# A two-layer encoder trunk on one core: first half of x scaled in two pieces, first two features' projections moved ahead of value products, value weights copied behind features

## The chip, the cores and the metric

The kernel runs on one core of a Trainium2 chip. A core has five engines with queues of their own: TensorE (PE in the profile; its weight loads are PEld), VectorE (DVE), ScalarE (ACT), GpSimd (POOL) and SyncE (SP, which issues nearly all transfers here). The metric is the device time of one execution in microseconds (us); smaller is better.

## The reference

Two layers act on x, 1024 positions by 1024 features, in float32. Each layer normalizes x, modulates it, mixes over positions, adds the result to x, and then does the same with a dense SwiGLU block. Only the start of layer 0 matters here:

```
mod = silu(c) @ ada_w[0] + ada_b[0]            # ada_w[0]: 1024 x 6144
sh1, sc1, g1, sh2, sc2, g2 = split(mod, 6)
h = rms_norm(x, norm1_g[0]) * (1 + sc1) + sh1
q, k, v, f_logit = split(h @ fox_w_in, ...)    # 1024 x (3*1024 + 16)
```

Forgetting attention with 16 heads follows, later gated linear attention, and a final normalization. So the first projections need the modulation vectors sh1 and sc1, and these need a third of ada_w[0], 8 MB.

## The kernel before, in words

The program is traced as straight code. A planner then orders the instructions of each engine by a simulated timeline, with the order of the code as priority; data dependences become semaphores. `tied(i, ...)` (L273) adds an order by hand: every instruction traced inside it stands behind `i` on `i`'s own engine. `last_of(e, n)` (L120) names the last instruction, or the one n before the last, traced on an engine so far. An instruction without such a tie stands wherever the planner put it.

Nearly all matrix products are done three times, on a high and a low part of each operand (`mm3`, L268): high times high, high times low, low times high. A weight is loaded raw, copied by ACT into its high part, and the low part is the difference, in four pieces (`split_w`, L208): piece i goes to POOL if i is below `lo_p` and to DVE otherwise.

"Features" below are the eight blocks of 128 columns of x. "Halves" are positions 0 to 511 and 512 to 1023. In the first stage this happens:

- `load_x`, `load_ada0`: SP issues x tiles (128 positions by 1024 columns, 512 KB), modulation weights (four transfers of 256 KB for each feature d) and projection weights into one queue. Order before: tiles 0 and 1, weights of feature 0, tiles 2 and 3, the f weight, q and k weights of the first head pair, modulation weights of features 1, 2 and 3, the first half of the value weights, modulation weights 4 and 5, the second half of the value weights, modulation weights 6 and 7, tiles 4 to 7.
- `ss_tiles` (L523): ACT squares tiles with a running sum, DVE and POOL turn the sums into 1/rms (`rstd`), and each tile is multiplied by it in place. `by` names the engine of each tile: D, A or G (POOL).
- `ada0_mod(d)` (L548): the modulation of feature d, a sum over eight chunks of 128 inputs. `NPE[d]` chunks are matmuls on PE (L557, each with one column); the others are summed on DVE (L563, L565) into `acc`, which PE reduces over partitions (L567). DVE adds the bias (L569, `modc`) and makes the multiplier (L410, `amul`).
- `h_block(d, hf)` (L573): PE transposes feature d of four tiles (L577), ACT applies multiplier and shift (L580, `y`) and makes the high part (L582), DVE or POOL makes the low part (L583).
- `first_k(d, hf, acc)` (L589): the products of feature d with the weights of f (two), q (three) and k (three), each over 512 positions, accumulated over the features in three PSUM banks.
- `first_v(d)` (L966): its twelve products with the value weights, 256 columns each, accumulated in two more banks.
- `pre(d)` (L976) is `ada0_mod`, the load for feature d + 3 and `h_block(d, 0)`.

The loop over d (L985) calls, for each d, the value weights' load and split (at d = 0 and 2), `pre(d + 1)`, `first_k(d)`, and, from d = 3 on, `first_v(d - 3)`; the second half's x tiles are loaded at d = 4 and squared and scaled at d = 4 and 5. Then the last value products, `first_evac(0)` and the second half's eight features follow. After that come value and q/k projections of further heads and attention, each on PE in turn.

Of the kernel before, what the change touches and what calls it, by code (L numbers as in the profile page):

```python
# [16 lines left out]
P = 128  # L17
# [37 lines left out]
def trunk(ctx, tc, x, c, ada_w, ada_b, norm1_g, norm2_g, ffn_w_in, ffn_w_out,  # L55
# [281 lines left out]
    def load_ada0(d):  # L337
        for kh in range(2):
            t = adr([P, 4, 2, P], F32, f"adas{d}{kh}")
            for j in range(2):  # L340
                with tied(*wv_ins if d > 3 else []):
                    nc.sync.dma_start(t[:, :, j, :], adaw[0, :, 4 * kh:4 * kh + 4, j, d, :])
                last_ada[:] = [last_of("S")]
# [179 lines left out]
    def ss_tiles(t0, n, by, ta=(), td=(), tg=(), late=()):  # L523
# [9 lines left out]
        for t, e in zip(range(t0, t0 + n), by):  # L533
            r = rstd[:, t:t + 1]
            if e == "D":
                nc.vector.tensor_scalar(xt[t], xt[t], r, None, op0=ALU.mult)
            elif e == "A":
                with tied(*late):
                    nc.scalar.activation(xt[t], xt[t], AF.Copy, scale=r)
            else:  # L540
                nc.gpsimd.tensor_scalar(xt[t], xt[t], r, 1.0, op0=ALU.mult, op1=ALU.mult)

    VLAG, XD = 3, 4
    NPE = (4, 4, 4, 2, 2, 2, 2, 2)

    mods = {}

    def ada0_mod(d):  # L548
# [3 lines left out]
        behind = [last_of("P")] if d == 1 else []  # L552
# [8 lines left out]
        for k in range(npe, 8):  # L561
            if k == npe:
                nc.vector.tensor_scalar(acc, part(k), cact[:, k:k + 1], None, op0=ALU.mult)  # L563
            else:
                nc.vector.scalar_tensor_tensor(acc, part(k), cact[:, k:k + 1], acc, op0=ALU.mult, op1=ALU.add)  # L565
# [327 lines left out]
    loads = v_loads(W, 2 * D)  # L893
# [64 lines left out]
    ss_tiles(0, 4, "DADG")  # L958
    scaled = last_of("D")
    with tied(last_of("A")):  # L960
        wf = split_w16(raw_f, "fw", wst)
        wq0, wk0 = (split_w(raw, 8, P, nm, wst) for raw, nm in zip(raw_qk, ("wq0", "wk0")))
    acc = first_acc(0)
# [12 lines left out]
    def pre(d):  # L976
        ada0_mod(d)
        if d + 3 < 8:
# [4 lines left out]
    done = {}  # L983
    pre(0)
    for d in range(8):  # L985
        if d == 0:
            feed.depth = 1
            wvs[0] = [feed.next()]
            wv_ins.append(last_of("S"))
        if d == 2:  # L990
            wvs[0].append(feed.next())
        if d < 7:
            pre(d + 1)
        first_k(d, 0, acc)
        if d >= VLAG:
            first_v(d - VLAG)
# [5 lines left out]
        if d == 4:  # L1002
            ss_tiles(4, 2, "GA", done[4]["A"], mods[5], done[4]["G"], done[5]["A"])
        if d == 5:
            ss_tiles(6, 2, "GA", done[5]["A"], mods[6], done[5]["G"], done[6]["A"])
            scaled2 = [last_of("A")]
# [8 lines left out]
    for d in range(8):  # L1015
        if d < 7:
            h_block(d + 1, 1)
        if d == 0:
            w_after.append(last_of("A"))
# [1234 lines left out]
```

## Time and profile before

| | |
|---|---|
| median of 3 runs | 2397.93 us (2396.83 to 2398.89) |
| profiled execution, its own time | 2394.36 us |
| its span in the profile | 2392.6 us |
| PE busy | 2356.5 us, 98% |
| DVE, ACT, POOL busy | 1678.7, 1190.1, 1198.1 us |
| HBM traffic | 269.25 MB read, 90.24 MB written |

All times in the profile count from the start of the span. A group "x8" in the timeline is a run of instructions of one line with the start of the first and the time from there to the end of the last. A matmul's duration includes a tail that overlaps the next matmul; the price of one in a row of matmuls is the distance of starts, which the chain of waits shows. The granted clock is the share of full speed that PE's throttle allowed in a stretch.

### The profile page before, as it was taken

Reading aid. Unit: us, or ns where it says so; the run is one execution under the profiler, and the core shown is the slowest. Engines: PE = TensorE matmul, PEld = TensorE weight load, DVE = VectorE, ACT = ScalarE, POOL = GpSimd, SP = SyncE. Lnnn points to the kernel's source line nnn. Section 1 sums busy time; section 2 is a strip of 40 time slices with the busy share of each in tenths; the row PEclk is TensorE's granted clock in tenths of the full one; section 3 lists DMA queues with packets and bytes.
Section 4 is the critical chain, followed back from the end, with each engine's and each line's share of the span. In section 5 each row is a group of like instructions: output and inputs, shape, how many; then the busy total and the mean of one; then the engine's idle time right before and its main releaser. Section 6 shows DMA issues by size and latency. Waiting matters only on the chain.

```text
span 2392.6 us, 35991 instructions
## 1 busy us (share of the span) xinstructions
PE 2356.5 (98%) x12286; PEld 2002.8 (84%) x12286; DVE 1678.7 (70%) x2797; ACT 1190.1 (50%) x2286; POOL 1198.1 (50%) x1070
## 2 busy tenths in 40 slices
PE   7999999999999999999999999999999999999998
PEld 6888888878888888888888898898888888888888
DVE  6577677676697778775788655345596766766787
ACT  5655556666554444434324766564443433345326
POOL 4234344432437778753363466563345666643262
PEclk9999999999999999999999999999999999999999
DMA  9233233133335555447665244454434534357664
GB/s 275 72 106 115 88 116 115 55 97 106 128 105 192 171 173 167 154 165 270 222 230 181 76 143 120 118 151 158 127 106 150 170 130 145 136 179 258 227 207 147
DMA packets 329408, 361.89 MB, mean 151 GB/s; under 512 B 24508, under 2 KB 253016, under 8 KB 329224
## 3 DMA queue, kind: packets, MB, share of 16 engines
q1 hardware_dynamic: 329032, 359.52, 46.5%
q8 instruction: 97, 1.59, 0.3%
q14 instruction: 87, 0.71, 0.1%
q10 hardware_dynamic: 192, 0.06, 0.0%
HBM read 269.25 MB, written 90.24 MB: 150 GB/s over the span
## 4 chain that ended last, share of the span: by engine, by line
PE 86%; ACT 3%; DVE 3%; DMA 3%; issue 2%; POOL 1%; SPq 1%; DVEq 0%; POOLq 0%; ACTq 0%
PE p_b L270 16%; PE p_b L269 16%; PE p_b L271 16%; PE o_b L1123 2%; PE t_b L1109 2%; PE qk_b L269 1%; PE qk_b L270 1%; PE qk_b L271 1%; PE s_b L1078 1%; PE s_b L1079 1%; PE gr_b L270 1%; PE gr_b L269 1%; PE gr_b L271 1%; PE vps_b L270 1%; PE vps_b L269 1%
## 5 line engine op out<-in xcount | busy, mean ns | idle before, releaser
L168 DVE TENSOR_TENSOR o_s<-xv_s,o_s 128x512 fp32r<-128x512 f32 (+1 forms) x376 | 343.1, 915 | 76.3 <-ACT o_s L167 75.5
L167 ACT CAST o_s<-xv_s 128x512 fp32r<-128x512 f32 (+1 forms) x376 | 218.8, 588 | 330.6 <-PE p_b L271 261.8
L1089 POOL TENSOR_SCALAR lp_s<-lp_s,st 128x128 f32<-128x128 f32 (+7 forms) x128 | 96.8, 761 | 294.3 <-DVE st L1088 251.9
L270 PE MATMUL p_b<-B,o_s 128*128 128x512 f32 x576 | 224.2, 389 | 0.0
L271 PE MATMUL p_b<-B,o_s 128*128 128x512 f32 x576 | 223.7, 389 | 0.0
L269 PE MATMUL p_b<-B,o_s 128*128 128x512 f32 x576 | 223.1, 389 | 0.0
L826 POOL TENSOR_TENSOR ex_s<-xv_s,xv_s 128x512 f32<-128x512 f32 (+1 forms) x64 | 87.2, 1362 | 252.1 <-DMA xv_s<-in_ffn_w_in_dram 88.7
L269 PE MATMUL p_b<-T,o_s 128*128 128x512 f32 x480 | 186.7, 389 | 0.0
L270 PE MATMUL p_b<-T,o_s 128*128 128x512 f32 x480 | 186.7, 389 | 0.0
L271 PE MATMUL p_b<-T,o_s 128*128 128x512 f32 x480 | 180.7, 389 | 0.0
L1087 ACT ACTIVATE lp_s<-lp_s,st 128x128 f32<-128x128 f32 (+7 forms) x128 | 99.5, 778 | 68.6 <-DVE st L1083 66.5
L270 PEld LDWEIGHTS p_b<-B,o_s 128*128 128x128 f32 x576 | 108.2, 188 | 22.4
L269 PEld LDWEIGHTS p_b<-B,o_s 128*128 128x128 f32 x576 | 108.1, 188 | 22.5
L271 PEld LDWEIGHTS p_b<-B,o_s 128*128 128x128 f32 x576 | 108.1, 188 | 22.3
L828 POOL TENSOR_TENSOR xv_s<-ex_s,xv_s 128x512 f32<-128x512 f32 (+1 forms) x64 | 85.5, 1335 | 59.6 <-DVE o_s L168 56.8
L167 ACT CAST pt_s<-t_b 128x512 fp32r<-128x512 f32 (+1 forms) x160 | 79.6, 547 | 69.3 <-PE t_b L1109 68.7
L1475 DVE TENSOR_TENSOR ex_s<-ex_s,p_b 128x512 f32<-128x512 f32 x140 | 94.1, 681 | 26.2 <-PE p_b L271 26.0
L220 POOL TENSOR_TENSOR w_l_s<-w__s,w_h_s 128x256 fp32r<-128x256 f32 x120 | 88.3, 767 | 48.2 <-ACT w_h_s L217 44.6
L168 DVE TENSOR_TENSOR pt_s<-t_b,pt_s 128x512 fp32r<-128x512 f32 (+1 forms) x160 | 96.6, 632 | 14.5 <-ACT pt_s L167 14.2
L447 POOL TENSOR_TENSOR ad_s<-ad_s,ad_s 128x512 f32<-128x512 f32 x62 | 88.3, 1425 | 35.1 <-ACT ad_s L445 22.7
L269 PEld LDWEIGHTS p_b<-T,o_s 128*128 128x128 f32 x480 | 90.1, 188 | 18.7
L270 PEld LDWEIGHTS p_b<-T,o_s 128*128 128x128 f32 x480 | 90.1, 188 | 18.7
(1999 smaller groups left out, 7502.2 us busy)
## 6 DMA issues: line engine op xcount, KB each, us to landing
xv_s<-in_ffn_w_in_dram SPq DMA_DIRECT2D x176, 256.0 KB, 3.2
hid_B<-x SPq DMA_DIRECT2D x70, 512.0 KB, 2.7
ad_s<-in_ada_w_dram SPq DMA_DIRECT2D x384, 64.0 KB, 2.0
hid_T<-x SPq DMA_DIRECT2D x36, 512.0 KB, 2.8
xv_s<-in_ffn_w_out_dram SPq DMA_DIRECT2D x96, 192.0 KB, 4.9
ada_s<-in_ada_w_dram SPq DMA_DIRECT2D x128, 128.0 KB, 2.6
xv_s<-in_ffn_w_out_dram SPq DMA_DIRECT2D x40, 256.0 KB, 2.8
T2o<-hid_T SPq DMA_DIRECT2D x18, 512.0 KB, 9.1
```

The source lines that it names most:

```text
L167: nc.scalar.copy(hi, src)
L168: nc.vector.tensor_sub(lo, src, hi.bitcast(F32))
L220: (nc.gpsimd if i < lo_p else nc.vector).tensor_sub(lo[:, cs], rw[:, cs], hi[:, cs].bitcast(F32))
L269: nc.tensor.matmul(ps, ah, bh, start=start, stop=False)
L270: nc.tensor.matmul(ps, ah, bl, start=False, stop=False)
L271: nc.tensor.matmul(ps, al, bh, start=False, stop=stop)
L447: nc.gpsimd.tensor_add(acc, acc, raw)
L826: nc.gpsimd.tensor_add(s1, a21, a22)
L828: nc.gpsimd.tensor_sub(a11, s1, a11)
L1087: nc.scalar.activation(lp, lp, AF.Exp, bias=mcur, scale=-1.0, accum_out=st[:, qi, 2:3])
L1089: nc.gpsimd.tensor_scalar(lp, lp, st[:, qi, 3:4], 1.0, op0=ALU.mult, op1=ALU.mult)
L1475: nc.vector.tensor_add(d, d if src is None else dest(G, src), ps)
```

## The change

1. Of tiles 0 to 3 only the first 256 columns (features 0 and 1) are scaled at first, by DVE, ACT, DVE, POOL as before. The other 768 columns follow in a new function `scale_x`: tiles 0 and 1 on ACT, 2 and 3 on POOL, behind feature 0 and behind the split of the k weights on these engines.
2. The splits of the q and k weights put two of four low pieces on DVE instead of one; the k weights are split after feature 0 instead of before.
3. Products of feature 0 are traced before `pre(1)`, those of feature 1 before `pre(2)`. The modulation matmuls of features 1 and 2 stand on PE behind the fifth-last PE instruction traced before them (the fourth of the eight products).
4. `NPE` of features 1 and 2 is 2 instead of 4. DVE's sum for a feature stands behind the sum of the feature before (for feature 1: behind feature 0's low part), and its third step behind that feature's `amul`.
5. The copies of the value weights on ACT stand behind feature 1 (first half) and feature 3 (second half). All four low pieces are on POOL. The load of modulation weights 4 is traced behind the first value load, and all loads of modulation weights are tied into one order.
6. The first value products stand on PE behind the products of feature 2.
7. The second half's x tiles are squared behind features 6 and 7 on ACT and scaled after that, by POOL, ACT, POOL, DVE (before: POOL, ACT, POOL, ACT, behind features 4 to 6).

```diff
@@ load_ada0
-                with tied(*wv_ins if d > 3 else []):
+                with tied(*wv_ins if d > 3 else [], *last_ada):
@@ ss_tiles
-    def ss_tiles(t0, n, by, ta=(), td=(), tg=(), late=()):
+    def ss_tiles(t0, n, by, ta=(), td=(), tg=(), late=(), first=D):
...
-        for t, e in zip(range(t0, t0 + n), by):
-            r = rstd[:, t:t + 1]
+        scale_x(t0, by, slice(0, first), late)
+
+    def scale_x(t0, by, cols, late=()):
+        for t, e in enumerate(by, t0):
+            x_, r = xt[t][:, cols], rstd[:, t:t + 1]
             if e == "D":
-                nc.vector.tensor_scalar(xt[t], xt[t], r, None, op0=ALU.mult)
+                nc.vector.tensor_scalar(x_, x_, r, None, op0=ALU.mult)
...
-    NPE = (4, 4, 4, 2, 2, 2, 2, 2)
-    mods = {}
+    NPE = (4, 2, 2, 2, 2, 2, 2, 2)
+    mods, summed = {}, []
@@ ada0_mod
-        behind = [last_of("P")] if d == 1 else []
+        behind = [last_of("P", 4)] if d in (1, 2) else []
...
             if k == npe:
-                nc.vector.tensor_scalar(acc, part(k), cact[:, k:k + 1], None, op0=ALU.mult)
+                with tied(*summed):
+                    nc.vector.tensor_scalar(acc, part(k), cact[:, k:k + 1], None, op0=ALU.mult)
             else:
-                nc.vector.scalar_tensor_tensor(acc, part(k), cact[:, k:k + 1], acc, op0=ALU.mult, op1=ALU.add)
+                with tied(*mods[d - 1] if d > 1 and k == npe + 2 else []):
+                    nc.vector.scalar_tensor_tensor(acc, part(k), cact[:, k:k + 1], acc, op0=ALU.mult, op1=ALU.add)
+        summed[:] = [last_of("D")]
@@ loads
-    loads = v_loads(W, 2 * D)
+    loads = [a + (ws, 4) for a in v_loads(W, 2 * D)]
@@ first stage
-    ss_tiles(0, 4, "DADG")
+    ss_tiles(0, 4, "DADG", first=256)
     scaled = last_of("D")
     with tied(last_of("A")):
         wf = split_w16(raw_f, "fw", wst)
-        wq0, wk0 = (split_w(raw, 8, P, nm, wst) for raw, nm in zip(raw_qk, ("wq0", "wk0")))
-    acc = first_acc(0)
+        wq0 = split_w(raw_qk[0], 8, P, "wq0", wst, 2)
...
-    def pre(d):
+    def pre(d, load=True):
         ada0_mod(d)
-        if d + 3 < 8:
+        if load and d + 3 < 8:
             load_ada0(d + 3)
...
+    feed.depth = 1
     pre(0)
+    summed[:] = [last_of("D")]
+    with tied(last_of("A")):
+        wk0 = split_w(raw_qk[1], 8, P, "wk0", wst, 2)
+    with tied(last_of("A"), last_of("G")):
+        scale_x(0, "AAGG", slice(256, D))
+    acc = first_acc(0)
+    first_k(0, 0, acc)
     for d in range(8):
+        if d == 1:
+            first_k(1, 0, acc)
+        if d < 7:
+            pre(d + 1, d > 0)
         if d == 0:
-            feed.depth = 1
+            w_after[:] = [last_of("A")]
             wvs[0] = [feed.next()]
             wv_ins.append(last_of("S"))
+            load_ada0(4)
         if d == 2:
+            w_after[:] = [last_of("A")]
             wvs[0].append(feed.next())
-        if d < 7:
-            pre(d + 1)
-        first_k(d, 0, acc)
+        if d > 1:
+            first_k(d, 0, acc)
+        if d == 2:
+            k2 = [last_of("P")]
         if d >= VLAG:
-            first_v(d - VLAG)
+            with tied(*k2):
+                first_v(d - VLAG)
...
-        if d == 4:
-            ss_tiles(4, 2, "GA", done[4]["A"], mods[5], done[4]["G"], done[5]["A"])
-        if d == 5:
-            ss_tiles(6, 2, "GA", done[5]["A"], mods[6], done[5]["G"], done[6]["A"])
-            scaled2 = [last_of("A")]
+        if d == 6:
+            ss_tiles(4, 2, "", done[6]["A"], mods[7], done[5]["G"])
+            ss_tiles(6, 2, "", done[7]["A"], mods[7], done[5]["G"])
+            squared = [last_of("A")]
+            scale_x(4, "GAGD", slice(0, D), squared)
...
-            w_after.append(last_of("A"))
+            w_after[:] = [last_of("A")]
```

More of the change, by code (lines that the diff above doesn't have):

```diff
@@ L532, in ss_tiles @@
             nc.gpsimd.tensor_tensor(rstd[:, cs], rstd[:, cs], mhalf[:, 0:n], op=ALU.pow)
-        for t, e in zip(range(t0, t0 + n), by):
-            r = rstd[:, t:t + 1]
+        scale_x(t0, by, slice(0, first), late)
+    def scale_x(t0, by, cols, late=()):
+        for t, e in enumerate(by, t0):
+            x_, r = xt[t][:, cols], rstd[:, t:t + 1]
             if e == "D":
-                nc.vector.tensor_scalar(xt[t], xt[t], r, None, op0=ALU.mult)
+                nc.vector.tensor_scalar(x_, x_, r, None, op0=ALU.mult)
             elif e == "A":
                 with tied(*late):
-                    nc.scalar.activation(xt[t], xt[t], AF.Copy, scale=r)
+                    nc.scalar.activation(x_, x_, AF.Copy, scale=r)
             else:
-                nc.gpsimd.tensor_scalar(xt[t], xt[t], r, 1.0, op0=ALU.mult, op1=ALU.mult)
+                nc.gpsimd.tensor_scalar(x_, x_, r, 1.0, op0=ALU.mult, op1=ALU.mult)
     VLAG, XD = 3, 4
-    NPE = (4, 4, 4, 2, 2, 2, 2, 2)
-    mods = {}
+    NPE = (4, 2, 2, 2, 2, 2, 2, 2)
+    mods, summed = {}, []
     def ada0_mod(d):
```

## The prediction

> **What bounds the kernel now.** I read the page first (busy shares, chain of waits), then the first 72 us: the table of stretches, the timeline of every engine, the chain of waits and the DMA issues. The change touches only the work of those 72 us.
>
> ```profile
> span 2392.6 us, 35991 instructions
> PE 2356.5 (98%) x12286; PEld 2002.8 (84%) x12286; DVE 1678.7 (70%) x2797; ACT 1190.1 (50%) x2286; POOL 1198.1 (50%) x1070
> PE 86%; ACT 3%; DVE 3%; DMA 3%; issue 2%; POOL 1%; SPq 1%; DVEq 0%; POOLq 0%; ACTq 0%
> ```
>
> PE is busy for 98% of the span and holds 86% of the chain, so PE runs its instructions one after another to the end, and what reaches it earlier is kept as long as nothing else becomes late. The exception is the beginning. Stretches of 3 us (columns: PE, PEld, DVE, ACT and POOL busy, granted PE clock, DMA share, GB/s):
>
> ```profile
> core 0: us, PE busy (x) PEld busy (x) DVE busy (x) ACT busy (x) POOL busy (x), PEclk, DMA share, GB/s
> 30.00:33.00 3.00, 2.98 (x11) 2.50 (x11) 2.75 (x4) 1.45 (x3) 3.00 (x4) 0.50 1.21 291
> 42.00:45.00 3.00, 1.77 (x5) 1.38 (x6) 2.86 (x6) 1.15 (x2) 1.50 (x1) 0.71 1.15 325
> 45.00:48.00 3.00, 3.00 (x16) 2.70 (x15) 2.86 (x9) 2.40 (x4) 0.00 (x0) 0.72 1.03 409
> 51.00:54.00 3.00, 3.00 (x26) 2.82 (x24) 2.89 (x4) 2.94 (x6) 2.90 (x3) 1.00 0.16 38
> ```
>
> PE does 11 instructions at clock 0.50 where it later does 26 at 1.00, and it idles at 42. DMA is full until 48 and nearly empty from 51. The timeline (start, duration, engine, line; the idle time before and its releaser in brackets) shows why features come late:
>
> ```profile
> 9.84 0.35 DVE L563 TENSOR_SCALAR acc<-adas_s,cact 128x256 f32<-128x256 f32 x1 [0.66 <-DMA adas_s<-in_ada_w_dram]
> 15.18 1.15 ACT L539 ACTIVATE xt_s<-xt_s,rstd 128x1024 f32<-128x1024 f32 x1 [1.34 <-POOL rstd L532]
> 15.18 2.29 DVE L536 TENSOR_SCALAR xt_s<-xt_s,rstd 128x1024 f32<-128x1024 f32 x2 [1.14 <-POOL rstd L532]
> 15.24 1.68 POOL L541 TENSOR_SCALAR xt_s<-xt_s,rstd 128x1024 f32<-128x1024 f32 x1
> 16.42 1.14 ACT L217 CAST wq0h_s<-wq_s 128x512 fp32r<-128x512 f32 x2
> 18.12 0.68 DVE L410 SCALAR_TENSOR_TENSOR amul<-modc,vec 128x1 f32<-128x1 f32 x1
> 18.43 3.41 PE L557 MATMUL mp_b<-cact,adas_s 128*128 128x1 f32 x16
> 18.89 0.78 ACT L580 ACTIVATE y_s<-xp_b,modc,amul 128x512 f32<-128x512 f32 x1 [0.30 <-DVE amul L410]
> 19.68 2.50 POOL L220 TENSOR_TENSOR wk0l_s<-wk_s,wk0h_s 128x256 fp32r<-128x256 f32 x3
> 19.71 0.62 ACT L582 CAST h0h<-y_s 128x512 fp32r<-128x512 f32 x1
> 21.52 1.21 DVE L583 TENSOR_TENSOR h0l<-y_s,h0h 128x512 fp32r<-128x512 f32 x1
> 22.45 0.78 PE L591 MATMUL fs_b<-h0h,fw_s 128*128 128x512 f32 x1
> 24.35 1.53 DVE L565 SCALAR_TENSOR_TENSOR acc<-adas_s,cact,acc 128x256 f32<-128x256 f32 x3
> 27.00 0.16 DVE L410 SCALAR_TENSOR_TENSOR amul<-modc,vec 128x1 f32<-128x1 f32 x1
> 29.00 1.14 ACT L217 CAST wv_0h_s<-wv_s 128x512 fp32r<-128x512 f32 x2 [8.68 <-DMA wv_s<-in_fox_w_in_dram]
> 30.64 3.24 DVE L565 SCALAR_TENSOR_TENSOR acc<-adas_s,cact,acc 128x256 f32<-128x256 f32 x3
> 32.00 0.78 PE L591 MATMUL fs_b<-h0h,fw_s 128*128 128x512 f32 x1
> 36.16 0.48 PE L591 MATMUL fs_b<-h0h,fw_s 128*128 128x512 f32 x1
> 40.45 1.05 PE L557 MATMUL mp_b<-cact,adas_s 128*128 128x1 f32 x8 [0.59 <-DVE modc L569]
> 43.23 0.79 PE L591 MATMUL fs_b<-h0h,fw_s 128*128 128x512 f32 x1 [1.28 <-ACT h0h L582]
> 46.99 0.69 DVE L583 TENSOR_TENSOR h0l<-y_s,h0h 128x512 fp32r<-128x512 f32 x1
> 70.82 0.50 PE L591 MATMUL fs_b<-h0h,fw_s 128*128 128x512 f32 x1 [0.38 <-ACT h0h L582]
> ```
>
> K(d) below means the eight products of feature d (two for f, three each for q and k); V(d) its twelve value products; mods(d) its modulation sums. L591 starts K(0) at 22.45, K(1) at 32.00, K(2) at 36.16, K(3) at 43.23, and K(0) of the second half at 70.82. Feature 0 is ready for PE at 20.33 (19.71 + 0.62), but PE is busy with the sixteen matmuls of mods(1). Feature 1 has its modulation at 27.16 (27.00 + 0.16), but ACT sits in front of the copy of value weights whose transfer lands at 28.98; only after that copy does it make feature 1.
>
> **The change, part by part.** I carry three marks: K(1), K(2) and the second half's K(0); the last decides what reaches the end.
>
> *First pieces of x.* DVE scales two tiles of 1024 columns in 2.29; a one-input DVE operation of 256 columns took 0.35, so two cost 0.70 and the tie behind them opens 1.59 earlier, at 15.9. A quarter piece on ACT I put at 0.35 too, between a quarter of its 1.15 and the whole. Then ACT copies the f weight (about 0.28, a 128-column piece of wq0's kind, bounded by nothing and half of 1.14) and wq0, to about 17.0; the k copies now stand behind. y 0.78 and h 0.62 follow: 18.4 instead of 20.33.
>
> *K(0) ahead of mods(1).* Four products of K(0) now precede mods(1), which shrinks from sixteen matmuls to eight. K(0) starts at about 18.5 instead of 22.45. The four matmuls' worth of weights move to DVE: two more scaled sums for each of features 1 and 2, 0.51 each (1.53 for three).
>
> *Feature 1.* DVE's low part of feature 0 takes 0.69 to 1.21, so it is done at 19.1 to 19.7. Two pieces of wk0's low part, now on DVE, cost 0.4 to 0.9 each (a third of 2.50 is the upper end, L563's width the lower). The sum of feature 1 is one scaling and five accumulations: 0.35 + 5 x 0.51 = 2.9 undisturbed. Beside a busy POOL three accumulations took 3.24, 1.08 each, and POOL is busy here until about 23.3, with two wk0 pieces and then the remaining 768 columns of two tiles (three quarters of 1.68, 1.26 each). So the sum ends between 22.9 and 25.2; PE's closing sum, the addition and amul add about 1.0, y and h 1.45. K(1) starts between 25.3 and 27.7, not 32.00. The remaining x pieces are needed first by feature 2's transposes and are done before these.
>
> *Feature 2.* Its sum may begin but waits for feature 1's modulation (23.9 to 26.2), then four accumulations. Queued behind that wait on DVE is nothing that PE needs sooner. Its matmuls wait for four of K(1). At half clock four products take 1.7, eight mods matmuls 1.05, the closing sum 0.6, the additions 0.35: 29.0 to 31.4. The value copy on ACT is now behind feature 1 but nothing keeps it behind feature 2; standing there it holds ACT until 30.15. Then y and h: K(2) starts at 31.6 to 32.9 with the copy in front, 30.5 without. I take 31.7: 4.5 earlier than 36.16.
>
> *From K(2) to the second half's K(0)* the trace took 70.82 - 36.16 = 34.7. PE's single prices at full clock are in the chain of waits:
>
> ```profile
> 52.95 0.79 PE mp_b L557 x8
> 53.74 0.45 PE mp_b L567 x4
> 65.31 0.23 PE ks_b L271
> 65.54 0.44 PE xp_b L577 x4
> 65.98 0.12 PE vps_b L972
> ```
>
> Work in it: K(2) to K(7) 48 x 0.23 = 11.0; 87 value products, 10.4; mods of four features 4 x 1.24 = 5.0; seven sets of transposes 3.1. That is 29.5, so about 5 are lost. The change adds the nine products of V(0) that used to run before K(2) and are now tied behind it: 9 x 0.12 = +1.1. It returns the idle 0.59 and 1.28 in front of K(3), because the second value copy is now behind feature 3, and the 1.7 that half the clock cost over the 3.4 us around 43 to 47: at most 3.6. I take 2.7, the idle and half of the clock, since PE will have a larger store of value products then.
>
> DMA does not stand in the way:
>
> ```profile
> 32.35 8.66 SPq L342 DMA_DIRECT2D adas_s<-in_ada_w_dram x8
> adas_s<-in_ada_w_dram SPq DMA_DIRECT2D x32, 256.0 KB, 5.6
> ```
>
> The last modulation weights are issued by 41.0 and land by about 46.6; with 2.9 for a sum and about 3 to the feature, K(7) could run from some 51, while PE, at 1.85 + 1.43 + 1.24 + 0.44 = 5.0 a feature from 31.7, reaches it at about 57. The queue keeps its order x, modulation weights, value weights; moving feature 4's load behind the value load writes out the order that it had. The four low pieces on POOL instead of three take 3.4, needed by V(0) only after K(2).
>
> *Second half of x.* All squares are now behind features 6 and 7, and so are the scalings.
>
> ```profile
> 47.01 1.06 ACT L527 ACTIVATE sq_s<-xt_s 128x1024 bf16<-128x1024 f32 x1
> 50.29 0.89 POOL L532 TENSOR_TENSOR rstd<-rstd,mhalf 128x2 f32<-128x2 f32 x1 [5.54 <-DVE rstd L530]
> 51.27 1.35 POOL L541 TENSOR_SCALAR xt_s<-xt_s,rstd 128x1024 f32<-128x1024 f32 x1
> ```
>
> Behind feature 7: two squares with their sums about 2.5, DVE 0.3, the root 0.89, one or two scalings on POOL at 1.35 to 1.68: 5.0 to 7.1 until the transposes can run. K(7), V(4) and V(5) cover 1.85 + 2.9 = 4.7, and PE usually stands some way behind feature 7. Between 0 and +2.4 (with a half-clock stretch +4.1); I take +0.6.
>
> Sum: -4.5 + 1.1 - 2.7 + 0.6 = **-5.5 us**. I let it reach the end whole: a PE at 98% carries it. Its own bounds: -3.3 + 1.1 + 0 + 4.1 = +1.9, and -5.7 + 1.1 - 3.6 + 0 = -8.2. The profiled execution took 2394.36 for its span of 2392.6; less 5.5 is 2388.9. The median 2397.93 lies 3.6 above that execution, so **2392.4**.
>
> **The rivals.**
>
> *PE never runs dry (faster).* If the copy slips behind feature 2 and PE has products all the time, work alone counts: 30.5 + 29.5 + 1.1 = 61.1 instead of 70.82, -9.7 us, 2388.2. For it: DMA and DVE leave room. Against: in the old trace the order on PE lost 5 us in this stretch, also where nothing was scarce.
>
> *The clock eats the gain (about the same).* Value products no longer fill the holes between K(0), K(1) and K(2). PE would fall to 0.50 around K(2), as it did at 30 to 33, for 3.4 us, +1.7, and the hole at K(3) would stay, +2.7: -5.5 + 4.4 = -1.1, 2396.8. The Trainium skill, "TensorE: Matmul & The Clock Gate", section "HAM oscillation — how this bites in real kernels", speaks against the change here: gaps above some 3.4 us between bursts put PE back to half clock, each burst anew. The trace agrees that the clock is halved around its thin stretches (0.50, 0.71, 0.72). Against it: mods(1), mods(2) and the transposes still lie in those holes, and none is as long as the old wait for K(1).
>
> *Late scaling of the second half (slower).* If the transposes of the second half stand on PE directly behind K(7), with V(4) to V(7) behind them, only 1.85 covers the 7.1: 5.3 idle and 1.7 of half clock, 7.0. With the early terms at their poor end (-3.3 + 1.1) the kernel is 4.8 slower, 2402.7; it decides once the wait there exceeds 6.1 (4.5 - 1.1 + 2.7). For it: the tie on these transposes names the last product of K(7), not the value products. Against: V(4) precedes them in program order, and roots of tiles 4 and 5 need only feature 6.
>
> **How the numbers follow.** This kernel's runs tell 0.2%, 4.8 us, from no change. The forecast holds with 0.50 (2390 to 2395; about two thirds of that beyond 4.8 us), the saturated PE 0.17, the clock 0.20, the late scaling 0.13 (spread around zero, most of it above; 0.10 beyond 4.8 us with orders on DVE or ACT that I can't see). Faster 0.33 + 0.17 = 0.50, slower 0.10, same 0.40. The range reaches from just below the saturated case, 2387, to just below the full late-scaling price, 2401.5.
>
> **What would show it.** Right: K(0) near 18.5, K(1) before 28 and K(2) at 30 to 33; no ACT wait for value weights in front of feature 1; mods(1) of eight matmuls inside K(0); K(3) without an idle gap; the second half's K(0) near 65. Wrong: DVE accumulations of over 1 us in a row around 20 to 25 pushing K(1) past 28; an ACT wait for value weights now in front of feature 2 well past 30; clock 0.50 after 31; an idle PE in front of the second half's transposes; or a shift at 65 that is gone by 130.

## The result, and the profile after

The changed kernel takes 2399.78 us (median of 22 runs, 2397.09 to 2402.64). The kernel before, timed beside it, takes 2395.39 us (22 runs; the three runs that the prediction had seen gave 2397.93). The ratio is 1.0018, 95% interval 1.0012 to 1.0025: the change costs 4.4 us where the prediction had it gain 5.5. The direction was wrong.

The profiled execution has a span of 2398.5 us against 2392.6, a time of its own of 2400.17 us, and PE is still busy for 98% of it. From the page of the changed kernel:

```profile
span 2398.5 us, 35971 instructions
PE 2360.7 (98%) x12270; PEld 2005.7 (84%) x12270; DVE 1676.5 (70%) x2802; ACT 1188.4 (50%) x2287; POOL 1201.0 (50%) x1072
```

The next fence is the timeline of the changed kernel, several engines in order of time (start, duration, engine, line; idle before and its releaser in brackets). L597 starts the eight products K(d) of a feature, L583 are transposes, L560 and L573 the modulation sums mods(d), L570 steps of DVE's sum, L575 and L586 what DVE and ACT make of them.

```profile
18.67 0.80 PE L597 MATMUL fs_b<-h0h,fw_s 128*128 128x512 f32 x1 [1.09 <-ACT h0h L588]
20.13 0.84 DVE L570 SCALAR_TENSOR_TENSOR acc<-adas_s,cact,acc 128x256 f32<-128x256 f32 x1
26.43 0.78 ACT L586 ACTIVATE y_s<-xp_b,modc,amul 128x512 f32<-128x512 f32 x1 [5.11 <-DVE amul L410]
28.03 0.78 PE L597 MATMUL fs_b<-h0h,fw_s 128*128 128x512 f32 x1
31.45 0.95 PE L560 MATMUL mp_b<-cact,adas_s 128*128 128x1 f32 x8
32.26 0.58 PE L573 MATMUL mp_b<-ones,acc 128*128 128x1 f32 x4
32.88 0.16 DVE L575 TENSOR_TENSOR modc<-mp_b,vec 128x2 f32<-128x2 f32 x1 [2.75 <-PE mp_b L573]
33.81 0.78 ACT L586 ACTIVATE y_s<-xp_b,modc,amul 128x512 f32<-128x512 f32 x1 [3.53 <-DVE amul L410]
35.41 0.78 PE L597 MATMUL fs_b<-h0h,fw_s 128*128 128x512 f32 x1
43.38 0.47 PE L597 MATMUL fs_b<-h0h,fw_s 128*128 128x512 f32 x1
...
63.03 0.40 PE L597 MATMUL fs_b<-h0h,fw_s 128*128 128x512 f32 x1
64.94 0.38 PE L583 MATMUL xp_b<-ident,xt_s 128*128 128x128 f32 x2
65.78 0.44 PE L583 MATMUL xp_b<-ident,xt_s 128*128 128x128 f32 x2 [0.46 <-ACT xt_s L542]
67.50 0.44 PE L583 MATMUL xp_b<-ident,xt_s 128*128 128x128 f32 x2 [1.28 <-POOL xt_s L544]
73.40 0.66 PE L583 MATMUL xp_b<-ident,xt_s 128*128 128x128 f32 x4 [0.43 <-ACT y_s L586]
```

K(0) and K(1) come 3.8 and 4.0 us earlier than before (22.45, 32.00). K(2) comes 0.75 earlier (36.16), K(3) 0.15 later (43.23), K(7) at 63.03 instead of 63.17. The early start of K(1) is spent in 15 us. Then the transposes of the second half wait twice for the scaling of x (65.78, 67.50), and the last product of the second half starts at 92.75 instead of 89.60.

The table of stretches shows what was spent (columns: PE, PEld, DVE, ACT and POOL busy with their instructions, granted PE clock, DMA share, GB/s). Before:

```profile
16.00:30.00 14.00, 12.90 (x61) 11.45 (x62) 10.48 (x20) 4.99 (x10) 7.27 (x10) 0.99 1.19 296
30.00:43.00 13.00, 11.34 (x65) 9.64 (x64) 10.16 (x20) 5.21 (x9) 5.92 (x7) 0.88 1.19 298
43.00:63.00 20.00, 19.77 (x125) 17.94 (x126) 12.38 (x28) 12.38 (x19) 8.36 (x8) 0.91 0.61 199
63.00:92.00 29.00, 28.62 (x174) 24.80 (x174) 12.94 (x19) 19.99 (x37) 7.14 (x7) 1.00 0.07 19
```

The changed kernel:

```profile
16.00:30.00 14.00, 11.59 (x40) 9.26 (x39) 12.46 (x25) 7.29 (x12) 7.10 (x8) 1.00 1.19 296
30.00:43.00 13.00, 12.26 (x64) 10.94 (x63) 8.46 (x18) 4.21 (x7) 7.02 (x10) 0.74 1.19 298
43.00:63.00 20.00, 20.00 (x143) 18.51 (x143) 11.50 (x28) 8.34 (x13) 5.44 (x7) 1.00 0.61 197
63.00:92.00 29.00, 26.35 (x137) 21.78 (x136) 11.40 (x18) 19.57 (x36) 9.16 (x10) 0.94 0.06 19
```

Read them as a ledger: what PE loses is its idle time plus half of the time at half clock in which it works. One thing is missing in the clock column. The trace has no clock before a first stretch at full speed, which begins at 26.2 us in the kernel before and at 31.0 in the changed one, and the table prints 1.00 there. The starts of the 512-column products tell what PE did: they lie 0.43 us apart at 28.6 as well as at 36, where the granted clock is 0.50, and 0.23 apart at 43.7, where it is 1.00. So PE ran at half up to that first stretch; the products lie so in every run of this case. From the changed kernel:

```profile
28.61 0.63 PE L269 MATMUL qs_b<-h0h,wq0h_s 128*128 128x512 f32 x1
29.04 0.63 PE L269 MATMUL ks_b<-h0h,wk0h_s 128*128 128x512 f32 x1
...
35.98 0.63 PE L269 MATMUL qs_b<-h0h,wq0h_s 128*128 128x512 f32 x1
36.41 0.63 PE L269 MATMUL ks_b<-h0h,wk0h_s 128*128 128x512 f32 x1
...
43.69 0.39 PE L598 MATMUL fs_b<-h0l,fw_s 128*128 128x512 f32 x1
43.92 0.40 PE L269 MATMUL qs_b<-h0h,wq0h_s 128*128 128x512 f32 x1
```

Between 16 and 43 us the kernel before loses 2.76 us of idle time (14.00 - 12.90 and 13.00 - 11.34) and 6.8 of clock (at half up to 26.2, and for 3.4 us from 29.6). The changed one loses 3.15 and 10.9 (at half up to 31.0, and for 6.8 us from 34.4): 4.5 us more, although 16 of its one-column sums have gone to DVE. That is where the early start went: K(0) came first because mods(1) was put behind it, and what PE had to do up to K(3) was done no sooner. From 43 to 63 the kernel before loses another 0.2 and 1.7 (from 43.3), the changed one nothing, and both reach K(7) at the same time. From 63 to 92 the changed one loses 2.65 of idle time against 0.38, and 1.7 of clock (68.6 to 72.0).

Counted from the end, the same PE instruction lies 3.1 to 3.9 us later than before at 91 to 99 us, 5.1 later at 108 (a half-clock stretch from 109.5 follows the wait for the gate sums there), 4.0 at 226, 5.7 at 306 and then 5.6 to 6.2 to the end. That is more than the 4.4 us of the medians: the profiled execution of the kernel before is one of its faster ones (2394.36 against 2395.39).

### The profile page after: what moved, and what is told of

It reads as the page before. It is cut to its first block, busy times and chain, and to the rows that moved or that the text cites. A ratio compares the mean times of both kernels' runs of the same rounds, so it can differ in the third digit from the quotient of the medians.

```text
span 2398.5 us, 35971 instructions
## 1 busy us (share of the span) xinstructions
PE 2360.7 (98%) x12270; PEld 2005.7 (84%) x12270; DVE 1676.5 (70%) x2802; ACT 1188.4 (50%) x2287; POOL 1201.0 (50%) x1072
## 4 chain that ended last, share of the span: by engine, by line
PE 89%; ACT 3%; DVE 3%; issue 2%; POOL 1%; DMA 1%; SPq 0%; POOLq 0%; DVEq 0%; ACTq 0%
PE p_b L271 16%; PE p_b L269 16%; PE p_b L270 16%; PE o_b L1144 2%; PE t_b L1130 2%; PE qk_b L269 2%; PE qk_b L271 2%; PE qk_b L270 2%; PE s_b L1099 1%; PE s_b L1100 1%; PE gr_b L270 1%; PE gr_b L271 1%; PE gr_b L269 1%; PE vps_b L269 1%; PE vps_b L270 1%
## 5 line engine op out<-in xcount | busy, mean ns | idle before, releaser
L168 DVE TENSOR_TENSOR pt_s<-t_b,pt_s 128x512 fp32r<-128x512 f32 (+1 forms) x160 | 96.9, 632 | 13.9 <-ACT pt_s L167 13.7
L269 PEld LDWEIGHTS p_b<-T,o_s 128*128 128x128 f32 x480 | 90.1, 188 | 18.7
L271 PEld LDWEIGHTS p_b<-T,o_s 128*128 128x128 f32 x480 | 90.1, 188 | 18.7
L270 PEld LDWEIGHTS p_b<-T,o_s 128*128 128x128 f32 x480 | 90.1, 188 | 18.6
```

Of the source, the lines that this page charges most:

```text
L168: nc.vector.tensor_sub(lo, src, hi.bitcast(F32))
L269: nc.tensor.matmul(ps, ah, bh, start=start, stop=False)
L270: nc.tensor.matmul(ps, ah, bl, start=False, stop=False)
L271: nc.tensor.matmul(ps, al, bh, start=False, stop=stop)
```

## The experiments

Each kernel was timed beside the kernel before on the same chip. The kernels of one group below share those runs; in the expectations "call" stands for group. "At half" means a granted clock of 0.50 in the profiled execution, or, ahead of its first clock, starts 0.43 us apart.

### First group: one part undone at a time

*Second half scaled early again.* From the changed kernel:

```diff
-        if d == 6:
-            ss_tiles(4, 2, "", done[6]["A"], mods[7], done[5]["G"])
-            ss_tiles(6, 2, "", done[7]["A"], mods[7], done[5]["G"])
-            squared = [last_of("A")]
-            scale_x(4, "GAGD", slice(0, D), squared)
+        if d == 4:
+            ss_tiles(4, 2, "GA", done[4]["A"], mods[5], done[4]["G"], done[5]["A"])
+        if d == 5:
+            ss_tiles(6, 2, "GA", done[5]["A"], mods[6], done[5]["G"], done[6]["A"])
+            scaled2 = [last_of("A")]
```

> The changed kernel, but the second half's x tiles squared and scaled behind features 4 to 6 as before (POOL, ACT, POOL, ACT). The changed kernel was 4.4 us slower than the one before (22 runs each). If the late scaling is the cause: no wait in front of the second half's transposes (1.74 us of idle in the changed kernel) and no half clock behind it (68.5 to 71.9), the stretch from K(7) to the end of the second half's projections shrinks from 29.7 us to about 26.4 as in the kernel before, and the time comes to about +1 us over the kernel before (ratio near 1.0005). If the early features (clock and order around K(2)) are the cause: the ratio stays near 1.0018.

Measured: 2398.71 us, ratio 1.0012 (1.0004 to 1.0021). K(2) at 34.61, K(3) 42.53, K(7) 62.79, so the beginning is as in the changed kernel; the second half's transposes no longer wait for x and its last product starts at 89.78. The late scaling costs 3.0 us at that place in this pair of profiles and 1.4 us by the ratios, whose intervals overlap. Undoing it doesn't bring the kernel back to before: its second half ends 0.2 us behind with six value products fewer done, its median is 2.7 us longer. Counted from the end of the profiles it lies 0.9 us behind at 92 us, 2.4 at 135 and 4.8 at 306, where it is at half for 6.8 us and the kernel before for 3.4. What costs the part between 92 and 235 us stays open.

*Late scaling alone*, in the kernel before: the same block exchanged the other way.

> The kernel before with the late squaring and scaling of the second half alone (POOL, ACT, POOL, DVE, behind features 6 and 7). If the late scaling is the cause: about +3.3 us over the kernel before (ratio 1.0014), with an idle PE in front of the second half's transposes. If it is not: within 1 us of the kernel before, PE having enough value products in store.

Measured: 2396.23 us, ratio 0.9999 (0.9991 to 1.0008). In the old beginning late scaling costs nothing that the interval can show: no wait stands in front of the second half's first transposes. PE reaches K(7) 2.4 us after feature 7 is ready there (59.44, 61.81), in the changed kernel 0.6 us after it (62.45, 63.03), and value products stand between and behind the transposes.

*Value products not tied behind K(2)*, in the changed kernel:

```diff
-            with tied(*k2):
-                first_v(d - VLAG)
+            first_v(d - VLAG)
```

> The changed kernel without the tie that holds the first value products behind K(2). In the changed kernel K(2) starts at 35.4 and PE's clock is halved from 34.4 to 41.2. If missing filler is what halves the clock: V(0) runs between K(1) and K(2), the clock stays at 1.00 from about 31, K(3) comes some 3 us before 43.4, and the time falls by up to 3 us from the changed kernel (ratio near 1.0006). If the tie guards against something else: PE now waits in its order for the value weights (landed at 29 in the kernel before, then copy and low parts to about 33), K(1) and K(2) are later by 1 to 2 us, and the time is the same or higher than 1.0018.

Measured: 2398.29 us, ratio 1.0012 (1.0003 to 1.0020). K(2) comes later (37.42), K(3) earlier (42.42) and K(7) at 60.28, 2.8 us earlier than in the changed kernel. At the second half's transposes, whose x isn't scaled yet, PE waits as in the changed kernel, and 2.2 of the 2.8 us are left at the second half's last product (90.53), 0.9 behind the kernel before. The timeline of this kernel:

```profile
60.28 0.50 PE L597 MATMUL fs_b<-h0h,fw_s 128*128 128x512 f32 x1 [0.72 <-ACT h0h L588]
63.56 0.44 PE L583 MATMUL xp_b<-ident,xt_s 128*128 128x128 f32 x2 [0.47 <-ACT xt_s L542]
65.28 0.44 PE L583 MATMUL xp_b<-ident,xt_s 128*128 128x128 f32 x2 [1.29 <-POOL xt_s L544]
```

*mods(2) ahead of the low products of K(1)*, in the changed kernel: the five products of K(1) with feature 1's high part, then mods(2), then the three with the low part.

```diff
-            first_k(1, 0, acc)
+            k1_high(acc)
         if d < 7:
             pre(d + 1, d > 0)
+        if d == 1:
+            with tied(*sums2):
+                k1_low(acc)
```

> The changed kernel with K(1) cut in two: its five products with the high part of feature 1 first, then the modulation sums of feature 2, then its three products with the low part. In the changed kernel all eight of K(1) came first and feature 2's modulation waited for PE until 32.9. If PE's order is what made feature 2 late: its modulation at about 30.5 to 31, K(2) at about 33 instead of 35.4, and the gain of about 2 us is kept to the end only if the clock is not halved meanwhile (ratio near 1.001). If the clock decides: K(2) earlier, but K(3) at 43 as before and the ratio near 1.0018.

Measured: 2399.33 us, ratio 1.0016 (1.0008 to 1.0025). mods(2) starts at 29.76 instead of 31.45, but the clock is at 0.50 from 25.9 to 39.6. Feature 2 is ready for PE at 34.23 instead of 35.24, and PE, at half clock, is busy with the low products, mods(3) and transposes until K(2) starts at 35.91. The time is that of the changed kernel within the interval. What the earlier place would be worth at full clock, this run doesn't tell.

### Second group: the planner's order, and the holes filled

The planner had laid out PE, DVE, ACT and POOL differently as far as 235 us into the program. Theory A took that for the cause, B denied it; C, D and E are about PE's clock and holes. To hold the old order, each engine's instructions behind `first_evac(1)` were chained by order-only dependences in the sequence of the kernel before:

```diff
+    for e, text in OLD_TURNS.items():
+        mine = [i for i in common if i.engine == ENG[e]]
+        ...
+        for p_, q_ in zip(turn, turn[1:]):
+            tc.add_manual_dep(mine[q_], mine[p_].name, mybir.DependencyInfo(
+                mybir.DependencyClass.NoSync, mybir.DependencyReason.DATA), reason="order")
```

> The changed kernel, with one thing held: from the point where the second half's projections are evacuated on (about 90 us into the program), the instructions of PE, DVE, ACT and POOL run in exactly the order that they have in the kernel before; the beginning is the changed one. Theory A (the planner, given an earlier beginning, laid out the attention stage in another and worse order, worth about 1.8 us between 99 and 133 us of the run with the early scaling): about 2398, ratio 1.0009, and the distance to the kernel before, counted from the end, no longer grows between 100 and 235 us. Theory B (the whole loss lies in the first 92 us, order is nothing): 2399.8, ratio 1.0017, as the changed kernel. A profile may show a half-clock stretch near 300 us of 0, 3.4 or 6.8 us, whichever theory holds.

Measured: 2399.4 us, ratio 1.0010 (1.0001 to 1.0019).

> As the last one, and the second half of x is scaled where the kernel before scales it (as in the run with the early scaling, 2398.7). So only the first 63 us are the changed ones. Theory A: the second half ends at about 89.8 us as in that run, against 89.6 before, and with the old order behind it nothing more is lost: 2396, ratio 1.0000 to 1.0004. Theory B: order is nothing, 2398.7, ratio 1.0012 as that run.

Measured: 2399.34 us, ratio 1.0010 (1.0001 to 1.0019). The first ratio is the one that theory A gave (1.0009), the second the one that B gave (1.0012; A at most 1.0004), and both intervals are wide enough for either. Against A speaks the first profile: counted from the end it lies 2.4 us behind the kernel before at 99 us, 4.0 at 108 and 4.5 at 235, where A expected no growth. So theory A is not borne out, but up to about 2 us for the order can't be excluded.

The fillers of the next two kernels are products whose results nothing reads:

```diff
+    FILL = {1: 8, 2: 12}
...
             nc.tensor.matmul(mp[:, j:j + 1], acc[:, j, :], ones, start=npe == 0, stop=npe == 0 or j == 1)
+        for _ in range(FILL.get(d, 0)):
+            with tied(last_of("P")):
+                nc.tensor.matmul(vacc[0][:, 0, :], hT[0].hi[:, 0:P], wq0.hi.rearrange("p k m -> p (k m)")[:, 0:256],
+                                 start=True, stop=True)
```

> The changed kernel with the order held as in the first of this call, and twenty idle products added on PE, whose results nothing reads (256 columns each, into the value accumulator before its first real product, which starts it afresh): eight behind feature 1's modulation sums and twelve behind feature 2's. Both places are holes in which PE waits for ACT and DVE in the changed kernel (25.9 to 27.3 and 32.8 to 34.6 us). Theory C (the thin stretch of one-column products and waits ahead of K(2) halves PE's clock for the 6.8 us behind it, and these 6.8 us do the work of 3.4): with the holes filled the clock stays at 1.00 from 25 to 45 us, K(3) starts 1 to 3 us earlier than at 43.4, and the time falls by 1 to 3 us against the first of this call. Rival D (K(3) and what follows are set by DVE's accumulations and not by PE): the clock stays up, K(2) and K(3) start where they did, and the time does not move. Rival E (the fillers only take time): K(2) 0.5 to 1.3 us later, the time 0.5 to 1.3 us longer.

Measured: 2397.92 us, ratio 1.0007 (0.9998 to 1.0016). Stretches of this kernel, then of the one without fillers:

```profile
30.00:43.00 13.00, 13.00 (x97) 12.25 (x96) 9.07 (x20) 4.37 (x7) 7.01 (x10) 1.00 1.18 299
43.00:63.00 20.00, 19.06 (x129) 16.86 (x128) 12.03 (x27) 9.71 (x17) 5.36 (x7) 1.00 0.63 197
```

```profile
30.00:43.00 13.00, 12.73 (x71) 11.20 (x70) 8.46 (x20) 4.14 (x7) 6.46 (x10) 0.80 1.19 298
43.00:63.00 20.00, 20.00 (x142) 18.29 (x141) 12.13 (x26) 9.65 (x16) 5.60 (x7) 1.00 0.62 198
```

Twenty products that do nothing made PE faster: the clock stays at 1.00 from 29.9 to 105 us (without them it is at half up to 21.7, from 25.1 to 31.9 and from 35.3 to 38.7), PE runs 97 instructions, twelve of them fillers, instead of 71 between 30 and 43 us, K(3) starts at 40.59 instead of 41.86, and the last product of the second half at 89.60 instead of 91.27. In the ledger from 16 to 43 us that is 2.9 us less of idle time (1.09 against 4.03) and 1.0 less of clock, for some 2.4 us of fillers. In this pair the holes cost more as idle time than by the clock. C holds for the stage; the medians differ by 1.5 us, less than the intervals can tell apart.

> The second of this call (early scaling, order held) with the same twenty products in the two holes. Theory A with C: 2393 to 2395, ratio 0.999, faster than both kernels; K(3) before 42 us. A with D: 2396, no difference to the second of this call. B with D: 2398.7.

Measured: 2397.63 us, ratio 1.0006 (0.9997 to 1.0015). No half clock between 30.7 and 105.8; K(7) at 62.21 after a wait of 1.97 us for ACT. The gain is again about 1.7 us, and the kernel is not faster than before, against the expectation of A with C.

### Third group: both parts undone, and PE loaded on purpose

F is the rival that the second half ends near 89.6 whatever precedes it.

> The changed kernel with three things put back or added: the second half of x scaled where the kernel before does it, the first value products no longer tied behind feature 2's eight products, and eight idle products in the hole behind feature 1's modulation sums (their results are read by nothing); the order behind 90 us is that of the kernel before, as in the second of the last call. What is left of the change is the early K(0) and K(1). Theory C (PE's ledger: from 22 us on PE is the bound, so what counts is its idle time plus half of the time at half clock): the holes between 25 and 35 us are filled with idle and with value products, clock 1.00 up to 60 us, K(3) by 41.5, K(7) before 60 and the second half's last product at 86 to 88.5 against 89.6 before: 2392.5 to 2395, ratio 0.9985 to 0.9995, faster than both kernels. Rival F (the second half is held by ACT's and DVE's work on its own features and ends near 89.6 whatever comes before it): 2396 to 2398, ratio 1.0000 to 1.0008.

Measured: 2395.21 us, ratio 1.0002 (0.9994 to 1.0011). The second half's last product starts at 86.95, against F; the time is not below that of before, against C. In this profile 6.8 us at half clock near 298 and 3.4 at 103.5 take the lead of 1.9 us (at 99 us) away.

The next kernel adds zero to the value accumulator:

```diff
         if d > 1:
             first_k(d, 0, acc)
+        for _ in range(8 if d in (4, 5, 6) else 0):
+            with tied(last_of("P")):
+                nc.tensor.matmul(vacc[0][0:80, 0, :], wf[:, d, 48:128],
+                                 wq0.hi.rearrange("p k m -> p (k m)")[:, 0:256], start=False, stop=False)
```

> The changed kernel with the old order behind 90 us (2399.4 in the last call) and 24 products more, which add zero to the value accumulator: eight behind each of K(4), K(5) and K(6), where its PE was never idle (20.00 of 20.00 us busy between 43 and 63 us). 256 columns each; in rows of this stage a product of that width starts 0.12 us after the last. Theory C (PE is the bound there): K(7) starts 24 times 0.12, that is 2.8 us, later, and the time is 2 to 3 us longer than without them: 2401.5 to 2402.5, ratio 1.002 to 1.0027. Rival D (DVE's accumulations pace the features, and PE's busy time there is only its queue filled with value products that could wait): K(7) later by less than 0.8 us, time 2399 to 2400.

Measured: 2398.33 us, ratio 1.0014 (1.0005 to 1.0022), the same as without the 24 products within the interval. From K(3) to K(7) it takes 21.39 us instead of 19.65: 1.7 later, between C's 2.8 and D's 0.8. But the second half's last product starts at 91.27 in both, because in the kernel with more work the scaled x is there when PE comes: 1.13 us idle from 63 to 92 instead of 2.68, and no half clock instead of 3.4 us. So in this pair what PE does between 43 and 63 us doesn't set the end: the added work fills the wait for the late x, and in this execution the clock stays up behind it.

> As the first of this call, but without the eight idle products. It tells what the filler is worth where value products may fill the later holes. Theory C: half-clock stretches come back in the first 45 us (6.8 us in all or more), K(3) 1 to 2 us later than in the first, time 1 to 3 us longer than it: 2395 to 2398. Rival F or D: the same time as the first within 0.5 us.

Measured: 2392.79 us, ratio 0.9993 (0.9984 to 1.0002), 2.4 us less than the first of this group, where C expected 1 to 3 more, though the intervals overlap: the fillers bring nothing once value products fill the holes. The clock is at 1.00 from 31.1 to 102.8.

### Fourth group: the planner free, and the wait at 100 us

> The changed kernel with two parts undone: the second half of x is scaled where the kernel before scales it, and the first value products are not tied behind feature 2's eight products. No order is held and nothing is added: the planner lays out all the rest for itself. If order is nothing (as the two runs with it held said), this is the third kernel of the last call again: K(7) at 60.0, second half's last product at 87.0, time 2392.8, ratio 0.999 to 0.9997, faster than both kernels. If the planner's own order costs after all, it is 1.5 us or more longer: 2394.5 or above, ratio 0.9998 to 1.0004.

Measured: 2394.32 us, ratio 0.9996 (0.9987 to 1.0005). The beginning is the expected one without any order held, and by its ratio (0.9993 with the order held) order is nothing, within the interval. Timeline on PE, then the stretches:

```profile
36.70 0.48 PE L597 MATMUL fs_b<-h0h,fw_s 128*128 128x512 f32 x1
41.70 0.48 PE L597 MATMUL fs_b<-h0h,fw_s 128*128 128x512 f32 x1
...
59.92 0.50 PE L597 MATMUL fs_b<-h0h,fw_s 128*128 128x512 f32 x1 [0.70 <-ACT h0h L588]
61.89 0.60 PE L583 MATMUL xp_b<-ident,xt_s 128*128 128x128 f32 x4
```

```profile
16.00:30.00 14.00, 11.53 (x40) 9.06 (x39) 12.41 (x23) 7.39 (x12) 7.31 (x8) 1.00 1.19 296
30.00:43.00 13.00, 13.00 (x98) 12.29 (x97) 8.13 (x17) 3.98 (x7) 6.09 (x9) 1.00 1.19 299
43.00:63.00 20.00, 19.10 (x128) 16.93 (x128) 13.82 (x30) 13.94 (x21) 9.42 (x10) 1.00 0.62 197
63.00:92.00 29.00, 27.43 (x163) 23.17 (x161) 12.85 (x20) 20.40 (x37) 6.67 (x7) 1.00 0.06 19
```

K(2) is later than in the changed kernel (36.70 against 35.41), and everything behind it is earlier. Between 30 and 43 us PE runs 98 instructions at 1.00 instead of 64 at 0.74: 24 value products have started before K(2) and 36 before K(3), where the changed kernel has 0 and 14. In the ledger from 16 to 43 us this kernel loses 2.47 of idle time and 7.3 of clock (at half up to 30.5), the changed one 3.15 and 10.9, so 4.3 more; it shows as 1.68 at K(3) and as 22 value products of 0.12, 2.6, that are already done. At K(7) the whole lead is there, 3.11 us. From K(7) to the second half's last product it needs 26.96 us, the changed kernel 29.72: 1.09 less idle time and 1.7 less of clock account for the 2.76. The 5.9 us at 90 us reach the end (7.8 there in this pair of profiles, 5.3 by the ratios of the medians).

All the profiles together bear out the ledger and the cause. Nine kernels have done the same 72 value products when K(7) starts: from 16 us to K(7), less what the ledger says they lost, they take 32.9 to 33.5 us, though K(7) lies between 59.9 and 64.0. And in the six kernels with the new beginning that keep the tie and have no fillers in the holes, PE is at half for the last time before K(7) at 38.7 to 41.2 us; in the seven that have value products or fillers there, at 28.4 to 32.3. Each is a single execution, but the two groups don't touch.

At the second half's last product the two undone parts add up: the tie undone brings 2.2 us, the early scaling 3.0, both 5.9. The ratio is 1.0018 with both parts in, 1.0012 with either one undone, 0.9996 with both undone, and only the last interval lies clear of the first; whether the two together do more than their sum the intervals don't tell. With the tie and no fillers K(7) lies at 61.5 to 64.0, with the tie gone at 59.9 to 60.6, but then the x that is scaled late isn't ready.

Last, six fillers, like those above, ahead of the two products that spread the gate sums over the partitions, in the last kernel of the third group:

> The third kernel of the last call (early scaling, value products not tied, order held; 2392.8, ratio 0.9993) with six idle products of 256 columns put on PE right ahead of the two products that spread feature gate sums over the partitions (their results are overwritten by the first of these two). There PE waited 0.79 us at 100.3 for the cumulative sum and then ran 2.1 us of products of 16 rows, and behind it the clock was halved from 102.8 to 106.2, which the kernel before does not show at this place: its lead of 1.89 us at 99 us fell to 0.30 at 108. Theory C (thin PE work in one stretch of the clock's grid halves the clock in the next): the idle time there is filled, the clock stays at 1.00 from 95 to 290 us, the lead at 108 us is 1.5 or more, and the time is 1 to 1.6 us less: 2391.3, ratio 0.9986 to 0.9989. Rival G (the products of 16 rows alone are thin enough): half clock as before, 2392.8, ratio 0.9993.

Measured: 2396.71 us, ratio 1.0004 (0.9995 to 1.0013). Timeline and stretches:

```profile
100.72 0.88 PE L1066 MATMUL cb_b<-h0h 128*128 128x256 f32 x6
101.67 1.98 PE L1068 MATMUL cb_b<-cum_s,ident 16*128 16x512 f32 x4
```

```profile
100.60:104.00 3.40, 3.33 (x16) 1.88 (x15) 3.40 (x8) 0.90 (x2) 0.00 (x0) 1.00 0.21 29
104.00:107.40 3.40, 3.40 (x18) 3.40 (x17) 2.43 (x10) 3.15 (x8) 0.69 (x2) 0.50 0.84 260
```

The wait is gone, PE is busy for 3.33 of 3.40 us, and the clock is halved all the same behind it. G holds in this execution: with 2 us of products over 16 rows in the stretch the clock didn't stay up. In the first kernel of this group the same products, 1.98 us from 100.98 on, have no half clock behind them. The beginning of this profile is also slower than that of the third group's last kernel, whose code is the same there: its lead at 99 us, ahead of the fillers, is 0.59 instead of 1.89, so 1.3 us of the difference to that kernel are not the edit's.

The kernel with both parts undone is the better version of the changed one, by intervals that lie apart. Whether it beats the kernel before is open: its span in the profile is 1.9 us (with the order held 1.6 us) below, its intervals reach 1.0005 and 1.0002.

## Why the prediction was wrong, point by point

By marks, against the kernel before: up to K(2) the sum had -4.5, and -0.75 was measured; from K(2) to K(7) it had 1.1 - 2.7 = -1.6, and +0.6 was measured (27.62 against 27.01); from K(7) to the second half's last product it had +0.6, and +3.3 was measured (29.72 against 26.43). Together -5.5 and +3.15. The mark that the prediction carried to the end, the second half's K(0), was forecast near 65; its first product started at 73.90 instead of 70.82. Three steps failed: the price of the tied value products, K(2) as a mark of what is kept, and the price of the late scaling.

- **First pieces, K(0), K(1).** Nearly right: K(0) at 18.67 for 18.5, and mods(1) is eight matmuls inside K(0). K(1) at 28.03 for 25.3 to 27.7: DVE's sum ran beside a busy POOL with 0.84 for its first steps and ended at 24.88, near the poor end of 22.9 to 25.2, and PE's closing sum with the additions took 1.5 us instead of about 1.0.
- **K(2), forecast -4.5, measured -0.75.** The working let mods(2) go behind four products of K(1), and the planner put it behind all eight. It also priced mods(2) and its closing sum at full clock, 1.05 and 0.6, beside products at half; at half they took 1.70 and 0.99 in the run that put them first, and there K(2) started at 35.91. And the step took K(2)'s start for a mark whose gain is kept. The kernel with both parts undone starts K(2) later than the kernel before and the changed one, and is the first of the three at K(3).
- **"+1.1", nine products of V(0) moved behind K(2).** This step had the mechanism wrong. It priced the nine as work that stays the same wherever it stands. Undoing the tie brings K(7) 2.8 us earlier (60.28 against 63.03), and 2.9 earlier with the early scaling (59.92 against 62.79). With the tie no full products were left for the holes ahead of K(2), and PE was at half up to 41.2 us instead of 30.5, except for one stretch of 3.4 us. The tie also held off what no kernel had done yet: 36 value products before K(3) were to be had and 14 ran.
- **"-2.7", the hole at K(3) returned.** The idle time in front of K(3) did go, and the second value copy did stand behind feature 3. The half-clock stretch didn't: it moved from 43 to 34 and doubled. That 1.7 at 43 was also not the old beginning's in every execution: the kernel with late scaling alone, which has that beginning, is at 1.00 from 34.9 to 298 us.
- **Late scaling, forecast +0.6 of 0 to +4.1.** It costs 2.8 to 3.0 at the second half: 1.1 of idle time, and 1.7 of clock in the changed kernel; that clock was lost in three of the six kernels that pair it with the new beginning. The cover named, K(7), V(4) and V(5), was not there: the transposes stood directly behind K(7), as that rival said.
- **Carried whole to the end.** True of what is left at 90 us; not of a lead at K(1). Of the 5.9 us at the end in the profiled pair, 3.15 stand at 92 us; most of the rest is half clock behind the gate sums at 109.5 (3.4 us) and near 304 (6.8 us against 3.4 at 299), which single executions have in different lengths.
- **The rivals.** "The clock eats the gain" named the right place, K(2), and the right cause, value products gone from the holes; the stretch was 6.8 us, not 3.4. Its argument against, that one-column sums and transposes would fill the holes, was wrong. The late scaling rival was right about the order on PE. I treated the two as exclusive with 0.20 and 0.13; they come together, and 3.4 for the clock and 2.2 more for the scaling take -5.5 to about zero. The 0.10 for slower was too small for that reason.

## What to carry to other kernels

Before you move work out of a hole, ask what filled the hole: on an engine that is busy for 98% of the time, products that ran while it waited cost little and kept its clock up, and tied to a place where it doesn't wait they are paid in full. Count such a stage as a ledger (idle time, half of the time at half clock, work already done) at a mark behind it, not by the start of its first items, and take the clock from the starts of like products where the table has none. An edit that costs nothing in one beginning (late scaling alone, 0.9999) can cost 3 us in another: try parts of a change alone, undo them alone, and undo them together.

## What the runs showed of the hardware

In these runs PE begins at half clock and first reached full clock at 21.5 to 40.0 us. After that, half-clock stretches begin on a fixed grid in each execution. The changed kernel, around the first one (its clock begins at 31.0; the 1.00 of the first line is an empty entry, and products there start 0.43 apart):

```profile
27.60:31.00 3.40, 3.40 (x11) 2.45 (x10) 2.46 (x4) 1.40 (x3) 2.68 (x3) 1.00 1.19 297
31.00:34.40 3.40, 2.90 (x23) 2.64 (x21) 1.45 (x4) 0.59 (x1) 2.70 (x5) 1.00 1.21 290
34.40:37.80 3.40, 3.16 (x12) 2.87 (x13) 2.63 (x7) 0.81 (x2) 0.00 (x0) 0.50 1.17 305
37.80:41.20 3.40, 3.40 (x12) 2.92 (x13) 3.26 (x7) 2.17 (x4) 1.53 (x2) 0.50 1.18 304
41.20:44.60 3.40, 3.40 (x26) 3.21 (x26) 2.00 (x5) 0.66 (x2) 2.99 (x4) 0.99 1.17 313
```

The stretches of this execution start at 34.4, 68.6 and 109.5, 10 and 22 times 3.41 us apart from the first, and last 3.4 or 6.8 us; in other kernels up to 13.7. The Trainium skill, "TensorE: Matmul & The Clock Gate", section "Part 1: The HAM clock gate (the "warmup" mystery)", gives a free-running window of 3413 ns; the trace agrees.

I had not expected that PE can be 2.90 of 3.40 us busy by the profile, as from 31.0 to 34.4, and still be halved next. What it ran there were twenty one-column sums behind the last products of K(1); in the kernel with the last fillers it was 3.33 of 3.40, 2 us of it products over 16 rows. No single wait in the stretch from 31.0 to 34.4 was longer than 0.5 us. So a high PE share in a profile does not say that the clock will hold.

Where the grid falls differs from execution to execution, and with it which thin stretch is caught: the same beginning had half clock up to 31.0 and from 34.4 in one kernel, up to 21.7 and from 25.1 and 35.3 in another, and up to 40.0 without a break in a third, with K(7) at 63.03, 61.51 and 64.00. Near 300 us, where PE waits in every kernel, it was at half for 3.4 us in some executions, for 6.8 in others, and in one not at all. So a difference of 1 to 2 us between two single profiles says little here; the medians and their intervals decide.
